# w_out of a hybrid decoder block by seven half-size products, with its weights in four blocks

## The chip, the cores and the metric

The kernel runs on one core of a Trainium2 chip. A core has five engines with queues of their own: TensorE (PE, matmuls into the accumulator banks of PSUM; its weight loads are shown as PEld), VectorE (DVE), ScalarE (ACT), GpSimd (POOL) and SyncE (SP, which here only issues transfers between DRAM and the on-chip memory SBUF). Each engine works through its instructions in the order in which they were written into its queue when the kernel was built; between engines they wait on semaphores. The metric is the device time of one execution in microseconds, the median of several runs.

## The reference

A trunk of two layers on 512 tokens of 1024 features, in float32. The part that matters is the end of the mixing half of a layer and the start of its feed-forward half:

```python
gates = jax.nn.sigmoid(gate_logits)
g_ssd, g_mla, g_gdn = jnp.split(gates, N_BRANCH, axis=-1)
mixed = g_ssd * (y_ssd @ w_ssd_out) + g_mla * (y_mla @ w_mla_out) + g_gdn * (y_gdn @ w_gdn_out)
h = x + mixed @ w_out
f = jnp.square(jax.nn.relu(rmsnorm(h, norm2_g) @ w_up)) @ w_down
return h + f
```

`mixed` is 512 x 1024 and `w_out` 1024 x 1024. The logits of the gates come from the projection of the normalised input `xn` by `w_in`. The other sizes: `w_up` 1024 x 4096, `w_down` 4096 x 1024.

## The kernel before, in words

**Products in three matmuls.** Every float32 product is made from halves: an operand is split into a high part, rounded to the format of the matmul (`fp32r`), and a low part, the rest. `mm3` issues high x high, high x low and low x high into one bank (L182 to L184 of the profile). Weights arrive from DRAM in pieces (`wraw`, two slots of 512 KB, for most matrices) and are split by `split_half`: ScalarE writes the high part `whi` (L154), VectorE the low part `wlo` (L155), 512 columns at a time, into four slots each. `split_half` has the planner's highest priority.

**Layouts.** Before `w_out` the features lie on the partitions: `mixed[d]` (tag `mix`) is a tile of 128 features x 512 tokens, d from 0 to 7. `dense_F` makes such tiles, `dense_T` makes tiles with tokens on the partitions, 128 tokens x 512 columns. `h`, four tiles of 128 tokens x 1024, is of the second kind.

**The output projections.** `out_proj` runs once for each of the three branches. For each of four `dp` it makes the gate's logits for 256 features from `xh`, `xl` (the split `xn`), takes the tanh into `cva` (L464), makes the branch's projection of the same 256 features from `yh`, `yl`, and adds the product to `mixed` (L472 and L473, VectorE). After branch 2, dp 3, `mixed` is complete. The last readers of `xh`, `xl` in this half are the gates of that dp, the last readers of `yh`, `yl` its projection.

**`w_out` before.** `mixed` is split into `mh`, `mlo`, which take the places `yh`, `yl` (L250 and L251). For two halves of 512 columns, `dense_T` runs eight k-tiles x four token tiles x three matmuls into four banks. The weights come through `wraw`. Evictions add half of a bank to `h` (L1115; the features of `mixed` carry a factor of 2 from the tanh form of the sigmoid) and ScalarE sums the squares for the norm (`square`, L271). In the second half of the columns the split weights are all held (`wh`, `wl`, in the pool `wo`), the token tiles are finished one after the other, and behind the third the first half of the norm (`norm_half`: `xr` L285, transposes L290, splits L254 and L255) is put in. The second half of the norm lies inside the first product of `w_up`.

**`w_down` before.** It has been made from seven products per quarter of its rows: with both sides cut into 2 x 2 blocks, four blocks of the activations (a11, a12, a22 and combinations s1 to s4) meet four blocks of weights (`wr00` to `wr11`, 1 MB each) and their sums p1 to p4. The forms of the activations are made in `up`, while `w_up` runs, and so are p1 and p3 (L1195). p2 and p4 are made beside the products (L1251, L1264). Each product has four k-tiles x two token tiles x three matmuls. Products share banks where their results add up, and after each VectorE adds to or subtracts from `h` (L1236).

**Order and places.** No order is written out by hand. A planner simulates the kernel when it is built, with costs and due times of its own, and appends to each engine's queue the instruction that is ready then, the earliest in the program (or the one with a raised priority) first. Tiles live in pools with fixed places. The long-lived pools (`lp` with `xh`, `xl`, `yh`, `yl` and `mix`; `wp` with `wraw`, `whi`, `wlo`) come first; above them the same space is used in turn by `ml` (attention), `br` (the other branches and `cva`), then `hp` (`h`) with `wo` (`w_out`) and afterwards `ff` (feed-forward) above it. `bp.close()`, which closes `br`, stands behind the last `out_proj`. On the chip a tile of such a pool waits only for those tiles whose place it takes (`reuse_waits="tile"`).

Of the kernel before, what the change touches and what calls it, by code (L numbers as in the profile page):

```python
# [10 lines left out]
F32 = mybir.dt.float32  # L11
# [9 lines left out]
P = 128  # L21
S = 512
# [33 lines left out]
def hybrid_kernel(ctx, tc, a, out, depth=2, taps=None):  # L56
# [30 lines left out]
    def acc_bank():  # L87
        return mk(ps_acc, [P, 512], F32, "acc")
# [159 lines left out]
    def split_act(hi, lo, src):  # L248
        with tc.high_priority(30):
            act.copy(hi, src)  # L250
            dve.tensor_tensor(lo, src, f32(hi), ALU.subtract)  # L251
# [99 lines left out]
    for ly in range(depth):  # L351
# [747 lines left out]
        h = mk(hpl, [P, T, D], F32, "h")  # L1099
        for t in range(T):  # L1100
            sync.dma_start(h[:, t, :], xsrc[t * P : (t + 1) * P, :])
# [6 lines left out]
        xh, xl = hilo_tags(lp, "x")  # L1108
        n2 = lambda i, pl, *tag: norm_half(i, hts, ssq, lambda k: col(g_n2 + k), pl, xh, xl, *tag)
        with tc.tile_pool(name="wo", bufs=1, reuse_waits="tile") as wo:  # L1110
            for c in range(2):

                def ev(t, ps):
                    hs_ = h[:, t, c * 512 : (c + 1) * 512]
                    dve.scalar_tensor_tensor(hs_, ps, 0.5, hs_, ALU.mult, ALU.add)  # L1115
                    square(ssq[t][:, c : c + 1], hs_, wo, "hj")
# [20 lines left out]
        with tc.tile_pool(name="ff", bufs=1, reuse_waits="tile") as fp:  # L1137
# [50 lines left out]

            def down_weights(qd):

                b = {}

                def plus(o, x, y):
                    for q in (slice(0, 1024), slice(1024, 2048)):
                        dve.tensor_tensor(o[:, q], x[:, q], y[:, q], ALU.add)  # L1195

                def after(c):
                    i, j = ((0, 0), (0, 1), (1, 1), (1, 0))[c]
                    b[i, j] = mk(fp, [P, 4 * 512], F32, f"wr{i}{j}")
                    rows, cols = (slice(o + 512 * e, o + 512 * (e + 1)) for o, e in ((qd * D, i), (0, j)))  # L1200
                    sync.dma_start(b[i, j].rearrange("p (k n) -> p k n", k=4), a["w_down"][ly][rows, cols].rearrange("(k p) n -> p k n", p=P))
                    if c == 2:
                        b["p1"] = mk(fp, [P, 4 * 512], F32, "wp1")
                        plus(b["p1"], b[0, 0], b[0, 1])
                    if c == 3:
                        plus(b[0, 1], b[0, 1], b[1, 1])

                return b, after

            def down(qd, ops, b):  # L1210

                x, z = ([acc_bank() for _ in range(2)] for _ in range(2))

                def product(ps, n, raw, start, i, j, op, done):  # L1220

                    w = []
                    for k in range(4):
                        w.append(split_half(raw(k)))
                        if done == 2 and qd == 3:
                            continue
                        for t in range(2):
                            mul(ps, n, w, k, t, start)
                    for t in range(2):
                        if done == 2 and qd == 3:  # L1230
                            for k in range(4):
                                mul(ps, n, w, k, t, start)
                        r = 2 * i + t
                        hs_ = h[:, r, j * 512 : (j + 1) * 512]
                        with tc.high_priority():
                            dve.tensor_tensor(hs_, hs_, ps[t], op)  # L1236
                        if done and qd == 3:
                            square(h_ssq[r][:, j : j + 1], hs_, fp, "fs", 3)
                            if done == 2:
                                finish(r, gb)  # L1240

                def mul(ps, n, w, k, t, start):
                    ah, al = (o[:, k % 2 * 256 + t * P : k % 2 * 256 + (t + 1) * P] for o in ops[n][k // 2])
                    mm3(ps[t], ah, al, *w[k], start and k == 0, k == 3, not start)

                b11, p3, b21, b22, p1 = (b[n] for n in ((0, 0), (0, 1), (1, 0), (1, 1), "p1"))

                halves = [mk(fp, [P, 2 * S], F32, "f", 4) for _ in range(2)]
                for q, o in enumerate(halves):
                    cs = slice(q * 1024, (q + 1) * 1024)  # L1250
                    dve.tensor_tensor(o, p1[:, cs], b22[:, cs], ALU.add)  # L1251
                gb = None
                if last and qd == 3:
                    gb = mk(fp, [P, D], F32, "f", 4)
                    sync.dma_start(gb, a["final_norm_g"].partition_broadcast(P))
                p2 = lambda k: halves[k // 2][:, k % 2 * 512 : k % 2 * 512 + 512]
                of = lambda o: lambda k: o[:, k * 512 : (k + 1) * 512]
                product(x, "a11", of(b11), True, 0, 0, ALU.add, 0)
                product([sm_bank() for _ in range(2)], "a12", of(b21), True, 0, 0, ALU.add, 1)
                p4 = p1  # L1260

                def plus4(q):
                    cs = slice(q * 1024, (q + 1) * 1024)
                    dve.tensor_tensor(p4[:, cs], halves[q], b21[:, cs], ALU.add)  # L1264

                product(x, "s2", p2, False, 0, 1, ALU.subtract, 0)
                product(z, "s1", of(p1), True, 1, 1, ALU.add, 0)
                plus4(0)
                product(x, "s3", of(p3), False, 1, 1, ALU.subtract, 1)
                plus4(1)  # L1270
                product(z, "s4", of(b22), False, 0, 1, ALU.add, 1)
                if qd == 3:
                    for t in range(2):
                        finish(t, gb)
                    if not last:
                        norm_half(0, hts, h_ssq, lambda k: params[0][:, 124 + k : 125 + k], fp, *nx, "f", 4)
                product(x, "a22", of(p4), False, 1, 0, ALU.add, 2)
            for qd in range(4):
                b, after = down_weights(qd)
                ops = up(qd, after)  # L1280
                if qd == 3 and not last:
                    nx = hilo_tags(lp, "x")
                down(qd, ops, b)
# [42 lines left out]
```

## Time and profile before

| | us |
|---|---|
| median of 3 runs (2316.47 to 2320.75) | 2317.59 |
| the profiled execution | 2320.83 |
| its span | 2319.1 |
| PE busy | 2283.2 |
| DVE busy | 1590.1 |
| ACT busy | 1177.4 |
| POOL busy | 59.0 |

The span runs from the first to the last instruction that the profile shows; the execution's time has 1.7 us more. Rows of the profile name line, engine, operation, and what is written from what (`out<-in`), with buffer numbers left out; `x32` counts instructions. In a timeline the first column is the start and the second the duration in us, and brackets show the idle time before an instruction and what ended it. For a matmul `out<-in` names first the moving operand and then the stationary one. In a table of windows the columns are length, busy time of PE, PEld, DVE, ACT and POOL with the number of instructions, PEclk (the clock that was granted to TensorE, 1.00 is full speed), the busy share of the DMA engines and GB/s. A row `SPq` is the issue of a transfer, not the transfer.

### The profile page before, as it was taken

Reading aid. Unit: us, or ns where it says so; the run is one execution under the profiler, and the core shown is the slowest. Engines: PE = TensorE matmul, PEld = TensorE weight load, DVE = VectorE, ACT = ScalarE, POOL = GpSimd, SP = SyncE. Lnnn points to the kernel's source line nnn. Section 1 sums busy time; section 2 is a strip of 40 time slices with the busy share of each in tenths; the row PEclk is TensorE's granted clock in tenths of the full one; section 3 lists DMA queues with packets and bytes.
Section 4 is the critical chain, followed back from the end, with each engine's and each line's share of the span. In section 5 each row is a group of like instructions: output and inputs, shape, how many; then the busy total and the mean of one; then the engine's idle time right before and its main releaser. Section 6 shows DMA issues by size and latency. Waiting matters only on the chain.

```text
span 2319.1 us, 32185 instructions
## 1 busy us (share of the span) xinstructions
PE 2283.2 (98%) x11858; PEld 1877.5 (81%) x11858; DVE 1590.1 (69%) x3132; ACT 1177.4 (51%) x2445; POOL 59.0 (3%) x74
## 2 busy tenths in 40 slices
PE   8999999999999999999999999999999999999998
PEld 7788787878887888888888877878788878888886
DVE  7777566866665558767867775668657645678668
ACT  6766744333443445554657666443334434545545
POOL 0000000000000000000000000000000000000000
PEclk9999999999999999999999999999999999999999
DMA  4223634442322443233132236334422224333231
GB/s 141 80 73 100 192 100 118 134 130 73 87 69 73 152 140 108 82 110 118 51 97 79 70 110 192 98 112 143 119 82 83 64 82 154 128 118 100 91 109 46
DMA packets 220158, 244.15 MB, mean 105 GB/s; under 512 B 34384, under 2 KB 172512, under 8 KB 220000
## 3 DMA queue, kind: packets, MB, share of 16 engines
q1 hardware_dynamic: 220000, 242.09, 34.4%
q8 instruction: 93, 1.52, 0.3%
q14 instruction: 65, 0.53, 0.1%
HBM read 225.60 MB, written 11.74 MB: 102 GB/s over the span
## 4 chain that ended last, share of the span: by engine, by line
PE 89%; DVE 6%; ACT 1%; DMA 1%; POOL 1%; issue 1%; SPq 0%; DVEq 0%; POOLq 0%; ACTq 0%
PE acc L182 23%; PE acc L183 23%; PE acc L184 23%; PE sm L182 2%; PE sm L183 2%; PE sm L184 2%; DVE wlo L155 1%; PE sm L751 1%; DVE tok L879 1%; PE sm L649 1%; DVE gQ L878 1%; PE sm L1036 1%; POOL gms L259 1%; ACT whi L154 1%; PE sm L760 1%
## 5 line engine op out<-in xcount | busy, mean ns | idle before, releaser
L155 DVE TENSOR_TENSOR wlo<-wraw,whi 128x512 fp32r<-128x512 f32 (+1 forms) x552 | 377.3, 687 | 406.0 <-ACT whi L154 399.1
L154 ACT CAST whi<-wraw 128x512 fp32r<-128x512 f32 (+1 forms) x552 | 340.3, 618 | 595.0 <-PE acc L183 414.6
L184 PE MATMUL acc<-xh,wlo 128*128 128x512 f32 (+1 forms) x1376 | 536.4, 390 | 0.0
L182 PE MATMUL acc<-xh,whi 128*128 128x512 f32 (+1 forms) x1376 | 535.7, 390 | 0.0
L183 PE MATMUL acc<-xl,whi 128*128 128x512 f32 (+1 forms) x1376 | 534.9, 389 | 0.0
L184 PEld LDWEIGHTS acc<-xh,wlo 128*128 128x128 f32 x1376 | 259.6, 189 | 49.4
L183 PEld LDWEIGHTS acc<-xl,whi 128*128 128x128 f32 x1376 | 259.6, 189 | 49.1 <-DVE xl L255 0.4
L182 PEld LDWEIGHTS acc<-xh,whi 128*128 128x128 f32 x1376 | 259.1, 189 | 49.4 <-ACT xh L254 0.4
L183 PE MATMUL acc<-yl,whi 128*128 128x512 f32 x384 | 151.4, 394 | 0.0
L182 PE MATMUL acc<-yh,whi 128*128 128x512 f32 x384 | 150.8, 396 | 0.0
L184 PE MATMUL acc<-yh,wlo 128*128 128x512 f32 x384 | 150.0, 391 | 0.0
L690 DVE SCALAR_TENSOR_TENSOR ckl<-acc,pc,ckl 128x511 f32<-128x511 f32 (+2 forms) x168 | 120.4, 743 | 15.4 <-ACT ckl L686 8.1
L154 ACT CAST whi<-wr 128x512 fp32r<-128x512 f32 x128 | 79.5, 621 | 66.6 <-PE acc L184 28.1
L184 PE MATMUL acc<-whi,yl 128*128 128x512 f32 x256 | 99.7, 389 | 0.0
L182 PE MATMUL acc<-whi,yh 128*128 128x512 f32 x256 | 99.7, 389 | 0.0
L183 PE MATMUL acc<-wlo,yh 128*128 128x512 f32 x256 | 99.6, 389 | 0.0
L155 DVE TENSOR_TENSOR wlo<-wr,whi 128x512 fp32r<-128x512 f32 x128 | 86.0, 686 | 12.1 <-ACT whi L154 11.4
L182 PEld LDWEIGHTS acc<-yh,whi 128*128 128x128 f32 x384 | 71.6, 188 | 16.1 <-ACT yh L254 1.7
L184 PEld LDWEIGHTS acc<-yh,wlo 128*128 128x128 f32 x384 | 72.2, 188 | 14.5
L183 PEld LDWEIGHTS acc<-yl,whi 128*128 128x128 f32 x384 | 72.2, 188 | 13.9
L454 ACT ACTIVATE eE<-eE,cum 128x128 f32<-128x128 f32 x192 | 63.2, 391 | 23.4 <-DMA eE<-d_c 23.4
L1236 DVE TENSOR_TENSOR h<-h,acc 128x512 f32<-128x512 f32 x96 | 61.6, 681 | 0.0
(429 smaller groups left out, 4418.3 us busy)
## 6 DMA issues: line engine op xcount, KB each, us to landing
wraw<-in_w_in_dram SPq DMA_DIRECT2D x144, 512.0 KB, 3.6
wraw<-in_w_up_dram SPq DMA_DIRECT2D x64, 512.0 KB, 3.6
wr<-in_w_down_dram SPq DMA_DIRECT2D x32, 1024.0 KB, 5.1
eE<-d_c SPq DMA_DIRECT2D x48, 256.0 KB, 4.1
wraw<-in_w_mla_out_dram SPq DMA_DIRECT2D x16, 512.0 KB, 3.3
eE<-d_e SPq DMA_DIRECT2D x32, 256.0 KB, 3.2
wraw<-in_w_ssd_out_dram SPq DMA_DIRECT2D x16, 512.0 KB, 3.4
wraw<-in_w_gdn_out_dram SPq DMA_DIRECT2D x16, 512.0 KB, 3.3
```

Source lines behind the costliest of these rows:

```text
L154: act.copy(hi, raw)
L155: dve.tensor_tensor(lo, raw, f32(hi), ALU.subtract)
L182: pe.matmul(o, ah, bh, start=start, stop=False, skip_group_check=more)
L183: pe.matmul(o, ah, bl, start=False, stop=False, skip_group_check=more)
L184: pe.matmul(o, al, bh, start=False, stop=stop, skip_group_check=more)
L259: pool.tensor_tensor(o, o, (exp if exp is not None else nhalf)[:, : o.shape[1]], ALU.pow)
L454: act.activation(o[:, i], o[:, i], AF.Relu, scale=-1.0, bias=cum[:, t, h0 + i : h0 + i + 1])
L649: pe.transpose(ps[:, n : n + P], pn[t][:, kb * P : (kb + 1) * P], ident)
L690: dve.scalar_tensor_tensor(acc[:, d:], ps[:, : S - d], taps_[3 - d], acc[:, d:], ALU.mult, ALU.add)
L751: pe.matmul(py[64 * i : 64 * i + 64, c * P : (c + 1) * P], xd[:, t, h * 64 : (h + 1) * 64], e2[h // 4][:, h % 4, :], start=True, stop=True)
L760: pe.matmul(po[:, c * P : (c + 1) * P], st[:, c * P : (c + 1) * P], ctl[:, tok], start=True, stop=True)
L1236: dve.tensor_tensor(hs_, hs_, ps[t], op)
```

## The change

`w_out` is made by the same seven products as a quarter of `w_down`. What was local to `w_down` becomes two functions, `seven_weights` and `seven`, which both matrices use; for `w_down` only the order in which `final_norm_g` is given its tile in the last quarter differs. For `w_out`:

- The weights no longer go through `wraw` but as four blocks of 1 MB into the pool `wo` (`wr00`, `wr01`, `wr11`, `wr10`, in this order, behind `h`), and p1 to p4 are made from them on VectorE.
- `mixed` is no longer split as such. `put` writes the halved high part on ScalarE and the low part on VectorE, for 256 tokens at a time; `comb` first makes a sum or difference on VectorE, in a tile `fc` of the pool `wo` (four slots). The forms a11, a12, a22 and s1 take the places `yh`, `yl`; s2, s3 and s4 take `xh0` to `xh5` and `xl0` to `xl5`. Neither raises its priority.
- The first half of the norm stands before the last product (a22), and the last product is run one token tile after the other.
- The pool `wo` no longer holds `wh`, `wl`.

```diff
-        mh, mlo = hilo_tags(lp, "y")
-        for d in range(KD):
-            split_act(mh[d], mlo[d], mixed[d])
...
+        def seven_weights(pl, w2d, r0):
+            b = {}
+            def plus(o, x, y):
+                for q in (slice(0, 1024), slice(1024, 2048)):
+                    dve.tensor_tensor(o[:, q], x[:, q], y[:, q], ALU.add)
+            def after(c):
+                i, j = ((0, 0), (0, 1), (1, 1), (1, 0))[c]
+                b[i, j] = mk(pl, [P, 4 * 512], F32, f"wr{i}{j}")
...
+                sync.dma_start(b[i, j].rearrange("p (k n) -> p k n", k=4), w2d[rows, cols].rearrange("(k p) n -> p k n", p=P))
+                if c == 2:
+                    b["p1"] = mk(pl, [P, 4 * 512], F32, "wp1")
+                    plus(b["p1"], b[0, 0], b[0, 1])
+                if c == 3:
+                    plus(b[0, 1], b[0, 1], b[1, 1])
+            return b, after
+        def seven(pl, ops, b, sq=None, before_last=None, fin=None, nf=4):
+            x, z = ([acc_bank() for _ in range(2)] for _ in range(2))
+            def product(ps, n, raw, start, i, j, op, done):
+                w = []
+                for k in range(4):
+                    w.append(split_half(raw(k)))
+                    if done == 2 and sq:
+                        continue
+                    for t in range(2):
+                        mul(ps, n, w, k, t, start)
+                for t in range(2):
+                    if done == 2 and sq:
+                        for k in range(4):
+                            mul(ps, n, w, k, t, start)
+                    r = 2 * i + t
+                    hs_ = h[:, r, j * 512 : (j + 1) * 512]
+                    with tc.high_priority():
+                        dve.tensor_tensor(hs_, hs_, ps[t], op)
+                    if done and sq:
+                        square(sq[r][:, j : j + 1], hs_, pl, "fs", 3)
+                        if done == 2 and fin:
+                            fin(r)
...
+            b11, p3, b21, b22, p1 = (b[n] for n in ((0, 0), (0, 1), (1, 0), (1, 1), "p1"))
+            halves = [mk(pl, [P, 2 * S], F32, "f", nf) for _ in range(2)]
+            for q, o in enumerate(halves):
+                cs = slice(q * 1024, (q + 1) * 1024)
+                dve.tensor_tensor(o, p1[:, cs], b22[:, cs], ALU.add)
...
+            product(x, "a11", of(b11), True, 0, 0, ALU.add, 0)
+            product([sm_bank() for _ in range(2)], "a12", of(b21), True, 0, 0, ALU.add, 1)
...
+            product(x, "s2", p2, False, 0, 1, ALU.subtract, 0)
+            product(z, "s1", of(p1), True, 1, 1, ALU.add, 0)
+            plus4(0)
+            product(x, "s3", of(p3), False, 1, 1, ALU.subtract, 1)
+            plus4(1)
+            product(z, "s4", of(b22), False, 0, 1, ALU.add, 1)
+            if before_last:
+                before_last()
+            product(x, "a22", of(p4), False, 1, 0, ALU.add, 2)
         with tc.tile_pool(name="wo", bufs=1, reuse_waits="tile") as wo:
-            for c in range(2):
...
-                hold = list(zip(*hilo_tags(wo, "w"))) if c == 1 else None
-                hook = (lambda t: t == 2 and n2(0, wo, "xr", 2)) if c == 1 else None
-                dense_T(weights(a["w_out"][ly], c * 512, 512, D, hold), 512, D, mh, mlo, ev, hook=hook)
+            b, after = seven_weights(wo, a["w_out"][ly], 0)
+            for c in range(4):
+                after(c)
...
+            def put(n, d, s):
+                hi, lo = (x[:, d % 2 * 256 : d % 2 * 256 + 256] for x in ops[n][d // 2])
+                act.mul(hi, s, 0.5)
+                dve.scalar_tensor_tensor(lo, s, 0.5, f32(hi), ALU.mult, ALU.subtract)
+            def comb(n, d, x, y, op):
+                s = mk(wo, [P, 256], F32, "fc", 4)
+                dve.tensor_tensor(s, x, y, op)
+                put(n, d, s)
+                return s
+            t0, t1 = ([m[:, hf] for m in mixed] for hf in HALVES)
+            for d in range(4):
+                put("a11", d, t0[d])
+                comb("s3", d, t0[d], t1[d], ALU.subtract)
+            for d in range(4):
+                put("a12", d, t0[d + 4])
+                s = comb("s1", d, t1[d], t1[d + 4], ALU.subtract)
+                s = comb("s2", d, s, t0[d], ALU.subtract)
+                comb("s4", d, t0[d + 4], s, ALU.add)
+                put("a22", d, t1[d + 4])
...
+            seven(wo, ops, b, ssq, lambda: n2(0, wo, "xr", 2), nf=2)
...
+                seven(fp, ops, b, *ends(qd))
```

More of the change, by code (lines that the diff above doesn't have):

```diff
@@ L1189, in down_weights @@
             def down_weights(qd):
[L1191 to L1251, printed above, removed]
@@ L1252, in down, with ends @@
+                return seven_weights(fp, a["w_down"][ly], qd * D)
+            def ends(qd):
+                if qd < 3:
+                    return None, None, None
                 gb = None
-                if last and qd == 3:
+                if last:
                     gb = mk(fp, [P, D], F32, "f", 4)
                     sync.dma_start(gb, a["final_norm_g"].partition_broadcast(P))
-                p2 = lambda k: halves[k // 2][:, k % 2 * 512 : k % 2 * 512 + 512]
-                of = lambda o: lambda k: o[:, k * 512 : (k + 1) * 512]
@@ L1258, in down @@
[L1258 to L1272, printed above, removed]
+                fin = lambda r: finish(r, gb)
+                def before_last():
                     for t in range(2):
[L1274 removed]
+                        fin(t)
                     if not last:
                         norm_half(0, hts, h_ssq, lambda k: params[0][:, 124 + k : 125 + k], fp, *nx, "f", 4)
[L1277 removed]
+                return h_ssq, before_last, fin
```

29 lines of the change are left out of this document (22 added, 7 removed).

## The prediction

> **What bounds the kernel now.** I read the page first (busy shares and the chain that ended last), then windows around `w_out`, then the timelines of TensorE, VectorE and the SP queue there, in the first of the two layers.
>
> ```profile
> span 2319.1 us, 32185 instructions
> PE 2283.2 (98%) x11858; PEld 1877.5 (81%) x11858; DVE 1590.1 (69%) x3132; ACT 1177.4 (51%) x2445; POOL 59.0 (3%) x74
> PE 89%; DVE 6%; ACT 1%; DMA 1%; POOL 1%; issue 1%; SPq 0%; DVEq 0%; POOLq 0%; ACTq 0%
> ```
>
> TensorE (PE) is busy nearly always and carries the chain. Fewer matmuls shorten the kernel, but only while nothing else makes PE wait.
>
> ```profile
> core 0: us, PE busy (x) PEld busy (x) DVE busy (x) ACT busy (x) POOL busy (x), PEclk, DMA share, GB/s
> 774.50:785.40 10.90, 10.90 (x49) 9.01 (x48) 6.99 (x12) 6.13 (x12) 0.00 (x0) 1.00 0.31 96
> 785.40:829.00 43.60, 43.60 (x202) 36.19 (x201) 24.23 (x45) 18.90 (x41) 1.67 (x3) 1.00 0.47 157
> 873.00:911.00 38.00, 38.00 (x169) 31.30 (x168) 34.00 (x52) 21.45 (x36) 0.00 (x0) 1.00 0.31 108
> 2312.00:2319.00 7.00, 0.00 (x0) 0.00 (x0) 3.05 (x6) 0.21 (x2) 0.90 (x2) 0.65 0.44 170
> ```
>
> The first row is the last output projection (`out_proj`, branch 2, dp 3), the second `w_out`, the third the first quarter of `w_down`, which has the seven products already. There VectorE (DVE) is busy 34.0 of 38.0 us and PE does not wait. But in `w_down` the forms and two of the four sums of blocks are made while `w_up` runs. The fourth row is the end of the kernel.
>
> ```profile
> 774.53 0.39 PE L182 MATMUL acc<-yh,whi 128*128 128x512 f32 x1
> ```
> ```profile
> 785.41 0.39 PE L182 MATMUL acc<-whi,yh 128*128 128x512 f32 x1
> ```
>
> The first is the start of the projection's 48 matmuls, the second that of `w_out`: 10.88/48 = 0.2267 us a matmul (the 0.39 of a row is latency). `w_out` follows without a gap, since its weights come through `wraw`, whose place is free early.
>
> **The change part by part.** *Matmuls.* Eight products of 24 become seven: 168 for 192 a layer, 24 x 0.2267 = **5.4 us less** if PE keeps its pace. Matmuls move to no other engine.
>
> *Where loads and forms can begin.* This decides the case. The four blocks, and the tiles `fc` that each combined form goes through, lie in the pool `wo`, which takes the place of `br`. `h` lies in `hp`, at the same place, and shows when such a pool opens:
>
> ```profile
> 770.44 17.24 SPq L161 DMA_DIRECT2D wraw<-in_w_out_dram  x4
> 787.73 1.90 SPq L1101 DMA_DIRECT2D h<-in_x_dram  x4
> ...
> 1919.37 17.24 SPq L161 DMA_DIRECT2D wraw<-in_w_out_dram  x4
> 1936.66 2.10 SPq L1101 DMA_DIRECT2D h<-hd  x4
> ```
> ```profile
> 775.88 0.37 SPq L161 DMA_DIRECT2D wraw<-in_w_out_dram  x1
> ```
> ```profile
> L1067 PE MATMUL yt<-ct,tok x32: 270/272/329, 606.5 to 725.3; 128*128 128x128 f32 x32
> L473 DVE TENSOR_TENSOR mix<-mix,cva x8: 681/690/693, 729.8 to 787.8; 128x512 f32<-128x512 f32 x8
> ```
> ```profile
> 786.00 0.68 DVE L472 SCALAR_TENSOR_TENSOR cva<-cva,acc 128x512 f32<-128x512 f32 x1
> 786.60 0.68 DVE L155 TENSOR_TENSOR wlo<-wraw,whi 128x512 fp32r<-128x512 f32 x1
> 787.20 0.68 DVE L251 TENSOR_TENSOR yl<-mix,yh 128x512 fp32r<-128x512 f32 x1
> 787.81 0.68 DVE L473 TENSOR_TENSOR mix<-mix,cva 128x512 f32<-128x512 f32 x1
> ```
>
> `x` lies in DRAM from the start, `br`'s large tiles (`tok`) are last read at 725.3, and SP only waits for `wraw` slots. Yet `h`, earlier in the program than `w_out`'s weights, is queued behind four of their loads, at 787.7, and in the second layer likewise. What ends then is the last reader of `cva`, also of `br`. So I read that the planner that writes each engine's order lets a pool open when the whole pool below is done: in its order every load of a block and every combined form stands behind that last addition. Without the two splits between, it ends near 787.
>
> *SP's queue.* The eight loads of `w_out` through `wraw` go; the next `w_up` loads take their slots (770.4 and, the single row, 775.9), and then stand `h` and the blocks. On the chip these wait for nothing, so they can start near 776, ahead of the planner's time:
>
> ```profile
> wr<-in_w_down_dram SPq DMA_DIRECT2D x4, 1024.0 KB, 9.2
> ```
> ```profile
> 834.00:838.00 4.00, 4.00 (x37) 4.00 (x35) 0.61 (x2) 0.86 (x2) 0.00 (x0) 1.00 1.05 409
> ```
>
> 2 MB of `h` and 4 MB of blocks at 409 GB/s are 15.4 us: the first block is in near 786 (2 us start, 3 MB), the last near 794. I cost transfers at nothing; cover is DVE's queue, below. Without it, started at 787.7, they would land near 797 and 805.
>
> *DVE's order.* How late does the planner think a block is in? The same blocks of `w_down` show it:
>
> ```profile
> 830.71 2.25 SPq L1201 DMA_DIRECT2D wr<-in_w_down_dram  x4
> ```
> ```profile
> 837.64 2.53 DVE L255 SCALAR_TENSOR_TENSOR xl<-sm,pc,xh 128x256 fp32r<-128x256 f32 x6 [3.39 <-ACT xh L254]
> 840.09 1.21 DVE L1195 TENSOR_TENSOR wp<-wr,wr 128x1024 f32<-128x1024 f32 x1
> ```
>
> The sum of the first two blocks stands behind six `xl`, though DVE sat idle 3.4 us before these: it expected the second block some 7 to 9 us after the first issue. With `h` first, I take 8 to 12 us after 787 for block one. In that time DVE is given the forms. Their number behind 787: 16 combinations (s1 to s4, four each), their 16 splits, and the splits of a12 and a22 for d = 2, 3, which need the last two features: 36 instructions of 256 columns. The eight other splits of a11, a12, a22 need no `fc` and replace six `yl` in the first window.
>
> ```profile
> L563 DVE TENSOR_TENSOR wlo<-wraw,whi 128x256 fp32r<-128x256 f32 x32 | 13.4, 418 | 7.3 <-ACT whi L561 6.7 <-PE acc L184 0.6
> L561 ACT CAST whi<-wraw 128x256 fp32r<-128x256 f32 x32 | 13.2, 412 | 10.7 <-PE acc L183 5.8 <-issue 3.8 <-PE acc L184 0.5
> ```
> ```profile
> 876.14 2.35 DVE L1251 TENSOR_TENSOR f<-wp,wr 128x1024 f32<-128x1024 f32 x2
> ...
> 882.86 1.28 DVE L1236 TENSOR_TENSOR h<-h,acc 128x512 f32<-128x512 f32 x2
> 884.06 1.29 DVE L155 TENSOR_TENSOR wlo<-wr,whi 128x512 fp32r<-128x512 f32 x2
> ```
>
> Pairs give the pace of successive instructions: 1.14 us for 1024 columns (2.35 less one of 1.21, as at 840.09), 0.60 for 512, so 0.34 for 256 (0.418 less the 0.08 by which a 512 one, 0.68, overlaps the next). Thus 36 x 0.34 = 12.2 us. ScalarE's 20 halves at 0.41 are 8.2 us beside it. Engines run their order as planned, so the first split of a block waits 8 to 12 us from 787 even if the block is in. PE, done at 785.4, starts at 795.5 to 800: a wait of 10 to 14.5; I take **11.5 us**, between the two.
>
> *Second wait.* Behind the four splits of a11 (2.4 us) DVE has the sum p1 (2.3), two additions to `h` (1.2), p3 (2.3) and half of p2 (1.1) before the splits of a12, whose block is loaded last: 9.3 us against 5.4 of matmuls. **4.0 us** taken, 0 to 5. From s2 on it is like `w_down`, 4 splits, 2 additions and at most one sum of half a block: 4.8 us for 5.4 of PE, no wait.
>
> *A check by DVE's sum* from 787: forms 12.2, sums 8 x 1.14 = 9.1, splits 28 x 0.60 = 16.8, 13 additions 7.8, and two `xr` with their small scalings, near 2.2: 48.1. So `w_out` ends at 835 at the earliest, with xl of the first norm half (8 x 0.42, from six in 2.53, = 3.4) at 838. Before, its last addition stood at:
>
> ```profile
> 830.95 0.69 DVE L1115 SCALAR_TENSOR_TENSOR h<-acc,h 128x512 f32<-128x512 f32 x1 [1.62 <-PE acc L184]
> ```
>
> So the layer loses at least 4 to 7 us whatever order DVE takes, as long as all this stands behind 787. That is the floor of my estimate.
>
> *Smaller edits.* The clock: the fourth window shows 0.65 as the mean after PE has stopped. A first product of 5.4 us at 0.65 costs 2.9; no row shows a start after such a wait, so 0 to 2.9, taken 1.0, near the bottom since most rows stand at 1.00. `w_up`'s first splits can no longer be made ahead: before, the second half of `w_out` held its own weights in `wo`, now the last product holds all four `whi` slots: 0 to 1.2 (two splits), taken 0.4. The last layer's `gb` takes its slot of `f` before the halves of p2: up to one 1.14, taken 0, as half two is wanted later. The moved `seven` for `w_down` issues what it did. Squares and norms stay in number.
>
> *Sum per layer:* -5.4 + 11.5 + 4.0 + 1.0 + 0.4 = +11.5; two layers **+23 us**. The profiled execution took 2320.8 (span 2319.1 and 1.7 around it) and would take 2344; the median of the runs shown is 3.2 lower, so **2341**.
>
> [...]
>
> **The rivals.**
> 1. *Loads and forms do begin during the gates* (other side: faster). `wo` would open tile by tile; then the 11 us of combined forms (32 x 0.34) and p1, p2, p3 lie in DVE's gaps before 785 (3.9 us idle in the first window alone), and DVE has no more to do in `w_out` than in the third window. PE waits 0 to 1.5: -5.4 to -3.9 a layer, **2308**. For it speaks that nothing on the chip makes a block wait after 725; against it `h`'s place, in both layers. It decides if the first block is issued before 776 in front of a `w_up` load and a combined form runs before 785.
> 2. *A shorter wait:* the planner expects block one soon, the splits come early and the forms fall between the products. DVE's sum remains: +4 to +7 a layer, **2330**. Against it the six `xl`.
> 3. *Transfers bound:* SP is held until 787.7; blocks land at 797 and 805, PE starts near 798 and again near 806 with products to catch up: 12.6 + 2.5 in place of 11.5 + 4.0, **2340**, by another cause.
> 4. *Worse:* each combined form goes DVE, ACT, DVE through four `fc` slots; if these leave DVE idle half as long as it works (6 us), +17 a layer, **2352**.
>
> **How the numbers follow.** Forecast 0.46, rival 1 0.12, rival 2 0.18, rival 3 0.12, rival 4 0.10; 0.02 for within 0.2% (4.6 us), about what a measurement of this kernel can tell from none. Faster 0.12, slower 0.86. The range, 2324 to 2353, leaves out rival 1 and the far ends of 2 and 4: it runs from 2317.6 + 2 x 3.2, below the floor of DVE's sum, to 2317.6 + 2 x 17.7.
>
> **What would show it.** In the changed profile: `h` and the four blocks on SP near 776; no combined form (`fc`) on DVE before 786; PE idle from 785.4 to near 797, put down to ScalarE's or DVE's split of the first block; a second gap of some 4 us before the products into `sm`; 168 matmuls; DVE near full from 787 to the end of `w_out`. If `fc` is written before 785, or PE starts below 790, the prediction is wrong.

## The result and the profile after

| us | before | after |
|---|---|---|
| median of the runs | 2317.03 | 2358.27 |
| lowest and highest | 2313.73 to 2320.75 | 2355.14 to 2359.67 |
| the profiled execution | 2320.83 | 2358.32 |

The kernel became slower: 1.0176 times the time before, 95% interval 1.0157 to 1.0194, or 41 us. The forecast was 2341 with a range to 2353. The sign and the mechanism were right, the size was not.

The head of the page of the kernel after (its span is 2356.5 us):

```profile
PE 2281.9 (97%) x11810; PEld 1871.6 (79%) x11810; DVE 1649.7 (70%) x3256; ACT 1204.1 (51%) x2509; POOL 59.5 (3%) x74
```

PE has 48 matmuls fewer, worth 10.9 us, and yet its busy time is nearly the same, 2281.9 for 2283.2: something made matmuls longer. PE also stands still for 39 us more (the span less PE's busy time: 74.6 for 35.9).

The waits of PE over the whole kernel after (total, count, longest); the first two groups do not exist before:

```profile
PE acc L182 <- ACT whi L154: 28.8, 3, 13.7
PE sm L183 <- DVE wlo L155: 6.4, 2, 3.2
```

Layer 1 from the end of the gates to the end of `w_out`, cut where PE starts again, and then the last stretch before that start (columns as in the prediction):

```profile
785.40:799.20 13.80, 0.10 (x1) 0.00 (x0) 13.59 (x39) 8.40 (x22) 0.00 (x0) 0.62 0.68 263
799.20:847.50 48.30, 44.66 (x182) 35.71 (x183) 39.39 (x61) 23.54 (x47) 1.93 (x3) 0.90 0.00 1
795.00:799.00 4.00, 0.00 (x0) 0.00 (x0) 3.85 (x12) 2.79 (x7) 0.00 (x0) 0.50 0.00 0
```

From 785.4 PE does nothing while DVE is busy 13.59 of 13.80 us, and afterwards the clock is below full in the mean (0.90). From 795 to 799 the DMA engines move nothing: the four blocks have landed. SP's queue and DVE's order around it:

```profile
776.22 1.96 SPq L1101 DMA_DIRECT2D h<-in_x_dram  x4
778.22 6.07 SPq L1117 DMA_DIRECT2D wr<-in_w_out_dram  x4
```
```profile
786.48 0.68 DVE L473 TENSOR_TENSOR mix<-mix,cva 128x512 f32<-128x512 f32 x1
787.08 0.41 DVE L1196 SCALAR_TENSOR_TENSOR yl<-mix,yh 128x256 fp32r<-128x256 f32 x1
787.41 1.09 DVE L1200 TENSOR_TENSOR fc<-mix 128x256 f32<-128x256 f32 x3
...
798.15 0.99 DVE L1196 SCALAR_TENSOR_TENSOR xl<-fc,xh 128x256 fp32r<-128x256 f32 x2
799.22 2.50 DVE L155 TENSOR_TENSOR wlo<-wr,whi 128x512 fp32r<-128x512 f32 x4
801.63 2.35 DVE L1111 TENSOR_TENSOR wp<-wr,wr 128x1024 f32<-128x1024 f32 x2
...
808.38 1.22 DVE L1161 TENSOR_TENSOR f<-wp,wr 128x1024 f32<-128x1024 f32 x1
809.52 1.89 DVE L155 TENSOR_TENSOR wlo<-wr,whi 128x512 fp32r<-128x512 f32 x3
```
```profile
798.58 2.16 ACT L154 CAST whi<-wr 128x512 fp32r<-128x512 f32 x4
```

The loads are issued at 776 and 778 while the gates still run. No combined form (`fc`) runs before the last addition to `mixed`. All forms come first, then the four splits of the first block, then p1, p3 and half of p2, then the splits of the second product. ScalarE has the same order: its high parts of the first block, which PE waits for, begin at 798.58, directly behind the high part of a form at 798.26. On PE the two restarts of each layer look like this:

```profile
799.24 0.79 PE L182 MATMUL acc<-whi,yh 128*128 128x512 f32 x1 [13.74 <-ACT whi L154]
810.26 0.79 PE L183 MATMUL sm<-wlo,yh 128*128 128x512 f32 x1 [3.20 <-DVE wlo L155]
1965.34 0.79 PE L182 MATMUL acc<-whi,yh 128*128 128x512 f32 x1 [13.74 <-ACT whi L154]
1976.96 0.80 PE L183 MATMUL sm<-wlo,yh 128*128 128x512 f32 x1 [3.20 <-DVE wlo L155]
```

A third price lies behind `w_out`. Its last addition to `h`, and the first one of `w_down`:

```profile
847.51 0.69 DVE L1146 TENSOR_TENSOR h<-h,acc 128x512 f32<-128x512 f32 x1
902.16 1.28 DVE L1146 TENSOR_TENSOR h<-h,acc 128x512 f32<-128x512 f32 x2
```

Before, these stood at 830.95 and 882.86. So `w_out` ends 16.6 us later and the first quarter of `w_down` begins to deliver 19.3 us later: 2.7 us more are lost between the two, in the handover to `w_up`.

### The profile page after: what moved, and what is told of

Same layout as the page of the kernel before. It is cut to its first block, busy times and chain, and to the rows that moved or that the text cites. A ratio compares the mean times of both kernels' runs of the same rounds, so it can differ in the third digit from the quotient of the medians.

```text
span 2356.5 us, 32291 instructions
## 1 busy us (share of the span) xinstructions
PE 2281.9 (97%) x11810; PEld 1871.6 (79%) x11810; DVE 1649.7 (70%) x3256; ACT 1204.1 (51%) x2509; POOL 59.5 (3%) x74
## 5 line engine op out<-in xcount | busy, mean ns | idle before, releaser
L155 DVE TENSOR_TENSOR wlo<-wraw,whi 128x512 fp32r<-128x512 f32 (+1 forms) x536 | 366.2, 686 | 388.0 <-ACT whi L154 380.9
L154 ACT CAST whi<-wraw 128x512 fp32r<-128x512 f32 (+1 forms) x536 | 330.5, 618 | 572.5 <-PE acc L183 411.3
L154 ACT CAST whi<-wr 128x512 fp32r<-128x512 f32 x160 | 98.8, 621 | 87.1 <-PE acc L184 44.2
L155 DVE TENSOR_TENSOR wlo<-wr,whi 128x512 fp32r<-128x512 f32 x160 | 107.0, 687 | 16.2 <-ACT whi L154 15.3
L184 PE MATMUL acc<-whi,yl 128*128 128x512 f32 x240 | 94.9, 395 | 0.0
L184 PEld LDWEIGHTS acc<-yh,wlo 128*128 128x128 f32 x384 | 72.2, 188 | 14.5
L183 PE MATMUL acc<-wlo,xh 128*128 128x512 f32 (+1 forms) x208 | 79.9, 384 | 0.0
L184 PE MATMUL acc<-whi,xl 128*128 128x512 f32 (+1 forms) x208 | 79.6, 383 | 0.0
```

Source lines behind the costliest of these rows:

```text
L154: act.copy(hi, raw)
L155: dve.tensor_tensor(lo, raw, f32(hi), ALU.subtract)
L183: pe.matmul(o, ah, bl, start=False, stop=False, skip_group_check=more)
L184: pe.matmul(o, al, bh, start=False, stop=stop, skip_group_check=more)
```

## The experiments

Theory A says that the time is lost by place and order: combined forms can be planned only behind the last reader of `br`, DVE then has the forms, the sums and the splits in one heap, PE waits twice and restarts at half clock. Its rival B says that the seven products of `w_out` cost more than they save wherever the forms are made, because DVE or the transfers have no room for them.

**Everything during the gates** (`e_full`). The last projection moves behind the closing of `br`, and its `cva` takes free places of the long-lived pool.

```diff
-                    t_ = mk(pl, [P, S], F32, "cva", 2)
+                    t_ = mk(pl, [P, S], F32, "cva", 2) if pl else mk(lp, [P, S], F32, f"ckh{len(tg)}")
...
-        out_proj(a["w_gdn_out"][ly], 2, *yg, br)
         bp.close()
...
         with tc.tile_pool(name="wo", bufs=1, reuse_waits="tile") as wo:
+            out_proj(a["w_gdn_out"][ly], 2, *yg, None)
             b, after = seven_weights(wo, a["w_out"][ly], 0)
```

> The pool br is closed before the last output projection, so that h, the four blocks, their sums and the forms can be planned during the gates; the last projection keeps its cva in ckh0 and ckh1. Theory A (the waits come from where the planner puts loads and forms): the wait of 13.7 us before the first product, the one of 3.6 us before the second and the slow clock behind both (4.4 us) go, the seventh fewer products stay: per layer -5.4 plus 2 us at the start of w_up, about 2310 us, faster than the kernel before. Theory B (VectorE's sum of work or the transfers bind w_out wherever they stand): TensorE still waits, and the time is not under 2335 us.

Measured: 2317.75 us (2315.08 to 2320.11), ratio 1.0000 (0.9991 to 1.0009). Its `w_out`, as a window, and the two additions as above:

```profile
784.30:824.90 40.60, 40.16 (x183) 32.75 (x182) 37.73 (x74) 26.07 (x56) 1.93 (x3) 1.00 0.00 1
824.87 0.69 DVE L1145 TENSOR_TENSOR h<-h,acc 128x512 f32<-128x512 f32 x1
879.53 1.28 DVE L1145 TENSOR_TENSOR h<-h,acc 128x512 f32<-128x512 f32 x2
```

The two waits and the slow clock are gone, and with them the whole loss of 40 us: A, not B, though the time is 7.8 us above A's 2310. `w_out` takes 40.6 us for 45.6 before (785.4 to 831.0), nearly the 5.4 of 24 matmuls. Yet the kernel is no faster than before. The handover takes 54.66 us (879.53 - 824.87), before 51.91: 2.7 us per layer are given back there. In this stretch PE waits three times for the norm, 1.4 us together, where the kernel before has no such wait; the two longer ones are:

```profile
825.97 0.50 PE L182 MATMUL acc<-xh,whi 128*128 128x256 f32 x2 [0.43 <-ACT xh L254]
827.30 0.63 PE L290 MATMUL sm<-ct,xr 128*128 128x128 f32 x4 [0.83 <-DVE xl L255]
```

The rest is work of PE that now lies behind the last addition (53.1 us busy for 51.8). Another wait, of 1.3 us for `whi` (L154), shows in the last `w_down`, as in the changed kernel.

**Loads early, forms late, twice.** The blocks get a pool `wq` opened before the gates, the forms' `fc` stays in `wo`, opened after them.

```diff
-        with tc.tile_pool(name="wo", bufs=1, reuse_waits="tile") as wo:
+        with tc.tile_pool(name="wq", bufs=1, reuse_waits="tile") as wq, ExitStack() as late:
+            with tc.tile_pool(name="cv", bufs=1, reuse_waits="tile") as cv:
+                out_proj(a["w_gdn_out"][ly], 2, *yg, cv)
...
+            wo = late.enter_context(tc.tile_pool(name="wo", bufs=1, reuse_waits="tile"))
```

> Only the loads and the sums of blocks are made early: the blocks lie in a pool of their own that opens before the last output projection, while the tiles fc of the combined forms stay in a pool that opens after it. Theory A, with the position of the first split as the cause: the splits of the first block no longer stand behind the forms, so the first product starts without a wait; the 12 us of forms then stand between the splits of the next products and cost a few us of waits: 2315 to 2325 us. If the forms themselves are the bound (VectorE's sum), the first wait only moves behind the first product: above 2335 us.

Measured: 2357.05 us (2354.11 to 2359.81), ratio 1.0168 (1.0154 to 1.0182), far from the 2315 to 2325 of A. But the edit had a second effect: `cv` opens only behind the unit before it, so that the gates no longer fill that unit's gaps, and PE waits there for `tok` (over the whole kernel 9.2 us, for 2.9 before):

```profile
PE yt L1067 <- DVE tok L1062: 4.6, 2, 4.1
```

That this is all of the difference is not shown. So the gates of dp 0 to 2 were given the free places of `e_full`, and only those of dp 3 lie in `cv` (`e_forms_late`).

```diff
-                out_proj(a["w_gdn_out"][ly], 2, *yg, cv)
+                out_proj(a["w_gdn_out"][ly], 2, *yg, {3: cv})
```

> The changed kernel with its h, blocks and block sums during the output gates, but the forms of the mixed features still in a place that opens only when the last unit's place is free, so after the gates; unlike the earlier run of this kind, the first three units keep their own places for the gates, so that the gates fill the same gaps as before. Theory A (two shares: the blocks and sums late, and the forms late): w_out starts on time, the wait at its start becomes that of the first forms alone, some 5 us instead of 13.7, w_out lasts about 53 us; about 10 us per layer less than the earlier run of this kind, 2337 us (2330 to 2343). Rival (the place of blocks and sums is worth nothing, the forms alone set the start): 2352 to 2358 us. Rival (the forms are covered): 2318 us.

Measured: 2341.70 us (2338.03 to 2342.34), ratio 1.0107 (1.0093 to 1.0121), A's 2330 to 2343. PE's waits in `w_out`:

```profile
PE sm L184 <- DVE yl L1198: 4.7, 1, 4.7
PE acc L182 <- ACT whi L154: 4.2, 1, 4.2
```

The forms being late costs 24 us (2341.70 - 2317.75), and the blocks and sums being late as well costs the other 17 (2358.27 - 2341.70). Neither alone explains the loss. Between this kernel and `e_full` it is mainly the place of the forms' tiles that differs.

**Only the place of `fc`** (`e_fc_early`): the combined forms go through tiles of the long-lived pool, and all else stays as in the change.

```diff
-                s = mk(wo, [P, 256], F32, "fc", 4)
+                s = mk(lp, [P, 256], F32, ("ckh0", "ckh1", "ckl0", "ckl1")[next(turn) % 4])
```

> Only the tiles fc are taken out of the late pool (they go to ckh0, ckh1, ckl0, ckl1); h and the blocks are still planned behind the last output projection. Some 22 instead of 36 instructions of forms stand behind the last addition to mixed. Theory A: the first wait shrinks from 13.7 us to the 22 x 0.34 us of these plus the additions before, 8 to 9 us; the second wait and the slow clock stay: about 5 us a layer less than the changed kernel, 2348 us. If the late loads are what holds the first product, nothing changes: 2358 us.

Measured: 2352.78 us (2348.34 to 2357.77), ratio 1.0151 (1.0131 to 1.0170). The first wait falls as expected, from 13.7 to 9.0; the second stays at 3.2:

```profile
PE acc L182 <- ACT whi L154: 9.0, 1, 9.0
```

The four runs spread over 9.4 us, so the total confirms no more than the direction.

**The clock alone** (`e_keep_clock`): 56 matmuls of the identity, into a bank that nothing reads, stand in the first wait.

```diff
+        keep = y_bank()
+        for _ in range(56):
+            pe.matmul(keep[:, :P], ident, ident, start=True, stop=True)
```

> The changed kernel with 56 matmuls of the identity, whose result nothing reads, put into the first wait (about 12 of its 13.7 us). If the slow first product comes from the clock that falls while TensorE idles, its 24 matmuls take 5.4 us instead of 7.2 and the granted clock is 1.00 there; the second product, behind another wait, stays slow at 7.8: 1.8 us a layer less, about 2354.5 us. If the slow pace has another cause (VectorE, ScalarE or memory), the first product stays at 7.2 us and the time at 2358 us or above.

Measured: 2355.63 us (2352.61 to 2356.96), ratio 1.0161 (1.0147 to 1.0174), by medians 2.6 us less than the changed kernel; the intervals of the two overlap. Windows over the first and the second product:

```profile
795.40:801.20 5.80, 5.77 (x24) 4.50 (x25) 5.17 (x7) 3.41 (x6) 0.00 (x0) 1.00 0.00 1
805.40:813.20 7.80, 7.05 (x18) 5.57 (x19) 4.93 (x8) 1.40 (x3) 0.00 (x0) 0.56 0.01 2
```

The first product now runs at full clock (1.00), 24 matmuls in 5.8 us. The second, behind its own wait, runs at 0.56. So each wait carries its own price. What is won at the first is not all kept: PE comes to the second wait earlier, and that grows from 3.20 to 4.25 us.

**The block of the second product earlier** (`e_b21_second`): the order of the loads becomes 00, 10, 01, 11.

```diff
-            def after(c):
-                i, j = ((0, 0), (0, 1), (1, 1), (1, 0))[c]
+            def after(c, order=((0, 0), (0, 1), (1, 1), (1, 0))):
+                i, j = order[c]
...
-                after(c)
+                after(c, ((0, 0), (1, 0), (0, 1), (1, 1)))
```

> The changed kernel with one edit: w_out's four blocks are loaded in the order 00, 10, 01, 11 instead of 00, 01, 11, 10, so that the second product has its block early; the forms are still made late and the first wait stays. Theory A (the second wait is the unread block's sum that stands behind the others on VectorE, and the slow clock of the second product comes from that wait): the wait of 3.6 us and the slow stretch of 2.6 us per layer go, both layers together about 12 us less than the changed kernel: 2346 us (2344 to 2350). Rival (the second slow stretch still belongs to the first wait, the clock only comes back late): the wait goes, the slow clock stays, 2351 us. Rival (VectorE's sum of forms is the limit and the wait only moves to a later product): 2355 to 2358 us.

Measured: 2361.09 us (2360.24 to 2364.10), ratio 1.0196 (1.0182 to 1.0210): A's 2346 missed, and a little over the third guess, that the wait only moves. It did move, from the second product to the third, whose weights now stand behind the same sums on DVE:

```profile
815.70 0.73 PE L182 MATMUL acc<-whi,xh 128*128 128x512 f32 x2 [3.24 <-ACT whi L154]
```
```profile
809.10 1.22 DVE L1111 TENSOR_TENSOR wp<-wr,wr 128x1024 f32<-128x1024 f32 x1
810.23 2.36 DVE L1111 TENSOR_TENSOR wr<-wr,wr 128x1024 f32<-128x1024 f32 x2
812.50 1.28 DVE L1146 TENSOR_TENSOR h<-h,sm 128x512 f32<-128x512 f32 x2
813.70 2.36 DVE L1161 TENSOR_TENSOR f<-wp,wr 128x1024 f32<-128x1024 f32 x2
815.97 2.50 DVE L155 TENSOR_TENSOR wlo<-f,whi 128x512 fp32r<-128x512 f32 x4
```

These rows follow each other without a break, up to 818.5. What sets the second wait is DVE's sum of work, not which block comes second.

**The handover.** Theory A for the gain that `e_full` gave back: the norm of the first two token tiles can begin only when the fourth sum product is added, and then one product (a22, 5.4 us) covers it; before the change two token tiles of the second half did, 10.9 us. So, in `e_full`, s4 is put ahead of s3, for `w_out` and `w_down` (`e_s4_first`).

```diff
-            product(x, "s3", of(p3), False, 1, 1, ALU.subtract, 1)
-            plus4(1)
             product(z, "s4", of(b22), False, 0, 1, ALU.add, 1)
+            plus4(1)
             if before_last:
                 before_last()
+            product(x, "s3", of(p3), False, 1, 1, ALU.subtract, 1)
             product(x, "a22", of(p4), False, 1, 0, ALU.add, 2)
```

> The version with everything of w_out made during the output gates, and in both users of the seven products the fourth sum product before the third, so that the first normalised token tile of the next step is ready two products, 10.9 us, ahead of its end instead of one, 5.4 us. Theory A (the gain of 24 matmuls per layer was given back at the start of w_up, because the norm of the first token tiles is covered by one product only): about 2.9 us per layer come back, 2312 us (2310 to 2315). Rival (the gain was given back in the planner's order of VectorE, not by cover): no change, 2317 us. Rival (the other token tile becomes late in its place): 2317 to 2321 us.

Measured: 2325.29 us (2322.93 to 2328.00), ratio 1.0041 (1.0028 to 1.0054): slower by 7.5 us, where 5 to 6 less were expected. With it ran `e_best`, the same with the final gain's load (`load_gb`) moved behind both halves of p2.

```diff
                 dve.tensor_tensor(o, p1[:, cs], b22[:, cs], ALU.add)
+            if halves_done:
+                halves_done()
...
-                return h_ssq, before_last, fin
+                return h_ssq, before_last, fin, 4, load_gb if last else None
```

> The version of the run before it, and the final gain's copy over all partitions is loaded after both halves of the third feature sum are made instead of ahead of them, so that it doesn't take their place in the last w_down. Theory A (in the last quarter a product waited 1.3 us for a form whose place the gain held): 1.3 us less than the version of the run before it, 2310 us (2308 to 2314). Rival (another form is late by as much in its place): the same as that version, within 0.5 us.

Measured: 2323.87 us (2319.98 to 2329.62), ratio 1.0030 (1.0015 to 1.0044). The difference of the two, 1.4 us, has the expected size, but their intervals overlap. The two largest waits of PE in `e_best` over the whole kernel; `e_full` has none of the first kind and 1.3 us of the second:

```profile
PE acc L182 <- DVE h L1145: 5.5, 10, 1.3
PE acc L182 <- ACT whi L154: 5.4, 7, 0.8
```

Both come from shared banks. s2, s3 and a22 use two banks (`x`), s1 and s4 two others (`z`). In the old order, s1, s3, s4, a22, a product with the other pair always stood between. In the new one s4 follows s1 and a22 follows s3, and each has to wait until the product before it has been added to `h`. In the first quarter of `w_down` of `e_best` (`fx` is the operand of s4, `yh` that of a22):

```profile
898.02 0.47 PE L182 MATMUL acc<-whi,fx 128*128 128x512 f32 x1 [0.54 <-DVE h L1145]
909.96 0.47 PE L182 MATMUL acc<-whi,yh 128*128 128x512 f32 x1 [0.77 <-ACT whi L154]
```
```profile
909.13 1.28 DVE L1145 TENSOR_TENSOR h<-h,acc 128x512 f32<-128x512 f32 x2
```

The profile puts the second wait down to a split, but ScalarE's first split for a22 was done at 905.8 and the first of the two additions of s3 ends near 909.8, so I read it as a wait for the addition too. The exchange was made at ten places (five in each layer), of which four have a norm or the end of the kernel behind them. Theory C was formed from the first of the two rows of waits, names only the pair s3 and a22, and was tried in two steps: the exchange only where a norm or the end follows (`e_norm_only`), and there with s3 done token tile by token tile, as a22 is (`e_row`; `e_norm_only` has `s3(False)` in the last line).

```diff
-            product(x, "s3", of(p3), False, 1, 1, ALU.subtract, 1)
-            plus4(1)
+            s3 = lambda rw: product(x, "s3", of(p3), False, 1, 1, ALU.subtract, 1, rw)
+            if not sq:
+                s3(False)
+                plus4(1)
             product(z, "s4", of(b22), False, 0, 1, ALU.add, 1)
...
+            if sq:
+                s3(True)
```

> The version of the last run, but the third sum product goes behind the fourth only where a norm or the end follows (w_out, and the last quarter of w_down), and not in the other three quarters of w_down. Theory C (what the exchange cost is that the third sum product and a22 then follow each other on the same two accumulators, so that a22 waits for the h adds of the product before it, about 1.5 us at every one of the ten places; what it gained is 2.9 us at each of three handovers): six of ten places lose their cost, some 9 us less than the version before it: 2315 us (2312 to 2317). Rival (the loss lies in the three norms themselves, which now stand in the way of the splits of the two products behind them): no change, 2323 us.

> The same, and where the third sum product stands behind the fourth it goes token tile by token tile, as a22 does already, so that the first accumulator is added to h while the second is still being filled, and a22 finds it free. Theory C: the last four places lose their 1.5 us too, 2310 us (2307 to 2313), under the time before. Rival (the four splits of the third sum product are then needed in half the time, 2.7 us instead of 5.4, and VectorE, which has the norm to do as well, can't deliver them): 2314 to 2318 us.

Measured: `e_norm_only` 2312.22 us (2308.81 to 2316.07), ratio 0.9978 (0.9970 to 0.9987); `e_row` 2310.08 us (2308.96 to 2312.45), ratio 0.9974 (0.9964 to 0.9984). The first lies in C's 2312 to 2317 at its low end, the second on its 2310; between the two the intervals overlap, so what the token tile order adds is not settled. Taking the exchange out of the other six places removes the waits of both pairs there, so these runs do not tell the two apart. The wait for `h` is 2.3 us at four places in `e_norm_only` and 1.2 us at four in `e_row`. Only one of them shrinks, the a22 at the end of the kernel, from 1.3 to 0.3; the others are s4 behind s1, and at the other three places a22 had no wait for `h`. So C's 1.5 us at each of the last four places is not what is seen.

The end of `w_out` with the first addition of `w_down` in `e_row`:

```profile
826.33 0.68 DVE L1146 TENSOR_TENSOR h<-h,acc 128x512 f32<-128x512 f32 x1
878.03 1.28 DVE L1146 TENSOR_TENSOR h<-h,acc 128x512 f32<-128x512 f32 x2
```

The handover is 51.7 us, as before the change (51.91). Part of the norm now lies inside `w_out`, which ends 1.5 us later than in `e_full`, so per layer 1.5 us are won by 878.03 for 879.53, not the 2.9 taken in the expectation. `e_row` is faster than the kernel before, by 0.26%. By medians it is 7.7 us faster than `e_full`, by the two ratios some 6; the two layers' 1.5 us and the gain's 1.3 give 4.3, and what the rest is was not followed.

## Why the prediction was wrong in size

**What bounds.** Right. PE carries the chain, and the change put waits into it.

**Pools and DVE's order.** Right in place and in length. `h` and the blocks on SP near 776 (776.22, 778.22), no `fc` before the last addition to `mixed`, 35 instructions behind it from 787.08 to 799.22 (of the 36 counted one split came ahead of it): 12.1 us for 12.2 worked out. `e_full`, in which the pool opens before the last projection, has none of the loss.

**First wait.** 13.74 in both layers against 11.5, inside 10 to 14.5. DVE was given all forms ahead of the first split, the upper end that the prediction had named. **Second wait.** 3.20 against 4.0, with the queue as listed: the additions, p3, half of p2. The slow first product hides a part of it: with that at full clock, in `e_keep_clock`, the wait is 4.25. Its cause is DVE's sum, since another order of the blocks moved it to the next product.

**The matmuls.** -5.4 worked out; `e_full` has 40.6 for 45.6 us.

**The step that failed** is the term of the clock, 1.0 us per layer. The working counted one wait and took a price near the bottom of 0 to 2.9, "since most rows stand at 1.00". Each layer has two restarts, and both pay. Windows of 0.2 us around the moments at which the clock changes in the two `w_out` of the kernel after:

```profile
788.60:788.80 0.20, 0.00 (x0) 0.00 (x0) 0.20 (x2) 0.20 (x2) 0.00 (x0) 0.86 1.13 440
802.20:802.40 0.20, 0.20 (x2) 0.14 (x1) 0.20 (x1) 0.00 (x0) 0.00 (x0) 0.51 0.00 0
809.20:809.40 0.20, 0.00 (x0) 0.00 (x0) 0.20 (x1) 0.00 (x0) 0.00 (x0) 0.56 0.00 0
816.00:816.20 0.20, 0.20 (x2) 0.20 (x1) 0.20 (x1) 0.00 (x0) 0.00 (x0) 0.88 0.00 0
1956.00:1956.20 0.20, 0.00 (x0) 0.00 (x0) 0.20 (x2) 0.20 (x1) 0.00 (x0) 0.75 1.05 410
1969.60:1969.80 0.20, 0.20 (x2) 0.15 (x1) 0.20 (x1) 0.00 (x0) 0.00 (x0) 0.61 0.00 0
1976.40:1976.60 0.20, 0.00 (x0) 0.00 (x0) 0.20 (x1) 0.00 (x0) 0.00 (x0) 0.95 0.00 0
1979.80:1980.00 0.20, 0.20 (x2) 0.20 (x1) 0.20 (x1) 0.00 (x0) 0.00 (x0) 0.52 0.00 0
```

Between these edges, and around them from 780 to 900 and from 1940 to 2050, the clock stands at 0.50 or 1.00. PEclk is the mean over the window, so the edge lies at a share of it: a fall that gives 0.86 happened after 72% of the window, at 788.74; the first return, 0.51, after 98%, at 802.40. From restart to full clock it took 3.2 us (799.24 to 802.40), 5.8 (810.26 to 816.05), 4.4 (1965.34 to 1969.76) and 3.0 (1976.96 to 1979.99). At 0.50 a matmul takes 0.43 us (eleven from 811.27 to 815.97), against 0.2267 at 1.00, so near half of this time is lost: as an estimate 1.6 + 2.9 = 4.5 us in layer 1 and 2.2 + 1.5 = 3.7 in layer 2, together 8.2 where 2.0 stood.

**The handover** was the second miss: 0.4 taken (0 to 1.2), for splits that come late; 2.7 measured. What PE waits for there is the norm (the rows of `e_full`), which only a22 covers, and not the splits of weights. `e_row`, which gives it two products, brings the handover back to 51.7, at the price of 1.5 us inside `w_out`.

**The final gain's slot:** 0 taken (up to 1.14), about 1.3 measured (the third wait for `whi` after: 28.8 - 2 x 13.74). `e_s4_first` still has a wait of 1.3 for `whi` and `e_best`, where the load stands later, has none above 0.8: the traces show the cause that the medians leave open.

The terms as measured: layer 1 has -5.4 + 13.7 + 3.2 + 4.5 + 2.7 = 18.7, layer 2 by the same handover 17.9, and with 1.3 for the gain 37.9. The prediction's +23 lacked 6.2 for the clock, 4.6 for the handovers, 4.4 for the first wait and 1.3 for the gain, and had 1.6 too much for the second wait: 14.9 in all. The range ended at 2353, which is 17.7 per layer.

The profiled executions differ by 37.5 (2358.32 - 2320.83), but that this is so near to 37.9 is in part chance. The clock also falls far from `w_out`, before:

```profile
504.00:512.00 8.00, 8.00 (x120) 6.30 (x114) 3.77 (x7) 6.06 (x11) 0.00 (x0) 0.57 0.90 207
1212.00:1220.00 8.00, 7.46 (x34) 6.13 (x35) 5.38 (x13) 3.56 (x7) 1.22 (x2) 0.79 0.15 48
1652.00:1660.00 8.00, 6.82 (x141) 5.18 (x140) 2.83 (x6) 4.54 (x8) 0.00 (x0) 0.79 1.04 196
```

Length times what PEclk lacks to 1.00 gives 3.4 + 1.7 + 1.7 = 6.8 us. The profiled execution of the kernel after has two such places, 64 to 70 and 504 to 510, both at 0.72, 3.4 us. Without these the difference is 40.9, near the 41.2 of the medians, and some 3 us of it are in none of the terms; what they are stays open.

**The rivals.** The first (loads and forms during the gates) did not happen; `e_full` made it happen and gave 2317.75, not 2308. The handovers (2 x 2.7) and the gain's slot (1.3) take back 6.7 of the 10.9 us that the matmuls save. In the profiled executions the other 4 us are seen (spans of 2315.0 and 2319.1), by medians they are not; the mean granted clock over the runs is 0.9963 in `e_full` and 0.9974 in the kernel before, which would be some 2.6 us, as an estimate, and the rest is open. The second is excluded by DVE's order. The third, transfers: `h` is issued at 776.22, not at 787.7, and the DMA engines move nothing from 795 on, before the first split of a block at 798.58, so they bound nothing. (For the 2 us of start the prediction names no row; on the page of the kernel before, loads of 512 KB into `wraw` land 3.3 to 3.6 us after their issue by medians, of which 409 GB/s make 1.3.) The fourth (gaps in DVE) is excluded by 13.59 busy of 13.80.

## What to carry to other kernels

Where an order is planned ahead, the place of a small tile can set the time of a large step: four `fc` tiles and four blocks in a pool that opens late cost 40 us, and the same arithmetic with other places was no slower than the kernel before. When products share accumulators, a new order must keep the other pair between them, for each pair, or the next product waits for the addition (`e_best`: 5.5 us in ten waits put down to it, and 5.4 in seven that I read so). Saved matmuls should be followed into the next step: what used to cover that step's first work may be what was saved.

## What the runs showed of the hardware

In layer 1 of the kernel after, a short gap cost more clock than a long one: 5.8 us at half clock behind 3.2 us of waiting and 3.2 us behind 13.7. The edges there, at 788.74, 802.40, 809.22 and 816.05, are 13.65, 6.83 and 6.82 us apart. Layer 2's, at 1956.10, 1969.76, 1976.58 and 1979.99, are 13.66, 6.82 and 3.41 apart. The kernel with the other order of blocks (`e_b21_second`) has its own edges,

```profile
787.00:787.20 0.20, 0.00 (x0) 0.00 (x0) 0.20 (x2) 0.20 (x2) 0.00 (x0) 0.59 1.05 410
804.00:804.20 0.20, 0.20 (x2) 0.10 (x2) 0.00 (x0) 0.00 (x0) 0.00 (x0) 0.74 0.00 0
```

at 787.04 and 804.10, 17.06 us apart. In these two profiles the distances are near one, two, four and five times the shortest of them, 3.41 us; no run shows why. The fall came at no fixed delay: 3.2 us after PE stopped in layer 1 of the kernel after (785.50 to 788.74), 4.5 us in layer 2 (1951.60 to 1956.10), 2.3 us in the kernel with the other order (784.77 to 787.04). Nor did the return: from a restart to full clock 3.0 to 5.8 us were seen. Once the clock even fell behind a restart: in the kernel with the other order PE starts again at 815.70, the clock falls at 817.76 (PEclk 0.89 in 817.60:817.80) and comes back at 821.17 (0.58 in 821.00:821.20), 3.41 us later. What makes the clock fall or return at these moments was not tried.
